# One weight pair in each of eight gate/up blocks: its low part made by an adding DMA or on GpSimd instead of on VectorE

## The chip, the cores and the metric

The kernel is one program on one core of a Trainium2 chip. The metric is the device time of one execution in microseconds (us). A run's time is a little longer than the span of the profiled execution, which goes from the first to the last recorded instruction.

## The reference

A block of a language model, 256 tokens by 2048 features, all in fp32: a feed-forward, a mixer, a second feed-forward, each with a norm ahead of it, a norm behind it and a residual addition.

```python
D_MODEL, SEQ, D_FF = 2048, 256, 5632

def _swiglu(x, w_gate, w_up, w_down):
    return (jax.nn.silu(x @ w_gate) * (x @ w_up)) @ w_down

def reference(x, ...):
    h = x
    f = _swiglu(_rmsnorm(h, ln_ffn1_pre), ffn1_gate, ffn1_up, ffn1_down)
    h = h + 0.5 * _rmsnorm(f, ln_ffn1_post)
    mx = _hybrid_mixer(_rmsnorm(h, ln_mix_pre), ...)   # rwkv7 scan + pooling
    h = h + _rmsnorm(mx, ln_mix_post)
    f = _swiglu(_rmsnorm(h, ln_ffn2_pre), ffn2_gate, ffn2_up, ffn2_down)
    return h + 0.5 * _rmsnorm(f, ln_ffn2_post)
```

The change touches only `x @ w_gate` and `x @ w_up` of the two feed-forwards.

## The kernel before

**Three products for one.** An fp32 product is made of three products of the type float32r. Each operand is split into a high part H (its value rounded to float32r) and a low part L (the value minus H), and `mm3` (L176 to L179) adds H·H, H·L and L·H: the lines L177, L178 and L179 of the profile. L178 is the one that needs the weight's low part.

**A weight's way.** Weights come in pairs: two rows of 128 by 512 columns, 512 KB, one tile of 128x1024. SyncE issues the load (`get_w`, L139), ScalarE casts the high part (`two`, L153), VectorE subtracts to get the low part (L154), and TensorE multiplies. The fp32 tile is one of four buffers (`w32`), the high and the low parts are in rings of five (`wH`, `wL`). Other tiles come from a pool of 33 larger buffers, `unit`.

**Order.** The program works with planned times. `put(t, fn)` appends matmul work that takes t to a list and moves the planned clock `clk`; `at(t, fn)` plans other work for a time; `run` replays both in the order of time. This fixes the order of the instructions on TensorE, ScalarE and VectorE; SyncE and GpSimd issue in the order in which `run` reaches their work. A pair is loaded at `slot(end)`: the planned end of the use that lies five ring entries back, so when its buffers come free. A matmul is planned at `MM` = 0.2265 us.

**A gate/up block.** The 5632 columns are done in 11 blocks of 512. Blocks 0 and 1 multiply plainly. Blocks 2 to 10 (`FAST`) go through `seven`, which saves matmuls by combining gate (called f, first) and up (l, last) weights: two rows of each give a "quad" of seven products in place of eight. A quad needs four loads of 256 KB (L372), three sums on VectorE (L377, L381, L385), casts on ScalarE (L392) and low parts on VectorE (L393). A block is three quads and ten plain pairs, in the order f6, f8, f10, quad, f12, f14, quad, then l6, l8, quad, l10, l12, l14 (the number is the pair's first row). That makes 183 matmuls, 41.5 us. Behind them come the merge (a copy on ScalarE, L416, and additions on VectorE, L419 and L435), the silu on ScalarE (L720) and the product with up on VectorE (L724). The result is turned in blocks of 32 on VectorE (L623), brought to its places by 16 transfers that GpSimd issues in the course of the next block (L635, `x<-T`), and split into high and low (L647, L651). Those transfers are GpSimd's only work in these blocks.

**The pair of the change.** It is l12, the last but one of a block. Its place among the engines' work around it, in order:

- TensorE: quad (second), l6, l8, quad (third), l10, **l12**, l14, next block.
- ScalarE and VectorE: cast and low part of l12 stand some 5 us ahead of its matmuls, behind those of l10.
- SyncE: its load follows the third quad's four loads and that of l10.

Of the kernel before, what the change touches and what calls it, by code (L numbers as in the profile page):

```python
# [11 lines left out]
F32 = mybir.dt.float32  # L12
F32R = mybir.dt.float32r
AF = mybir.ActivationFunctionType
ALU = mybir.AluOpType
# [3 lines left out]
P = 128  # L19
# [18 lines left out]
MM, MC = 0.2265, 0.12  # L38
# [9 lines left out]
        (2, 8, ((2, 4, 6, 8, 10, 12), (0, 2)), TRAIL))  # L48
OUT = ((0, 0, (), 0), (1, 2, ((4,), (0,)), 0), (3, 0, (), TRAIL))
FAST = range(2, 11)  # L50
CARRY = (18, 21)
NG, SPOTS = 3, ((2, 4), (1,))

# [5 lines left out]
class Block:  # L59
# [197 lines left out]
    def sums(s, T, out, when, own=None, nq=2):  # L257
# [62 lines left out]
        for i, fn in enumerate((first, second) + ((parts, lows) if own is not None  # L320
                                                  else (third, fourth))):
            s.at(when + 1.7 * i, fn)

    def seven(s, wf, cf, wl, cl, at, KT, T, sm, n, spots, ev_first, ev_last, trail=0,
              one_end=False, ends=(-0.05, 2.7)):


        nc = s.nc
# [15 lines left out]
        def rows(k, h):  # L344
            xH, xL = at(k)
            return xH[:, h * P:h * P + P], xL[:, h * P:h * P + P]
        ws = {}

        def keep(tiles):
            ws.update((k, (wH, wL)) for k, wH, wL in tiles)  # L350

        def pair(k, w, c0, b):
            s.at(s.slot(s.clk + 12 * MM), lambda: keep(s.load_w(w, k, 2, c0, 512)))

            def do():
                for i in range(2):
                    for h in range(2):
                        mul(f"{b}{h}", rows(k + i, h), ws[k + i])
            s.put(12 * MM, do)
# [265 lines left out]
    def carry_at(s, T1, T, t, x32=None):  # L625
# [34 lines left out]
        for h in range(2):  # L660
            s.at(t + CARRY[h], lambda h=h: high(h))
            s.at(t + CARRY[h] + 2, lambda h=h: low(h))

# [30 lines left out]
    def sumsq(s, src, acc):  # L694
        s.nc.scalar.activation(out=s.rtmp("junk").bitcast(mybir.dt.bfloat16), in_=src, func=AF.Square, accum_out=acc)

    def ffn(s, wg, wu, wd, uT, rs, gpost, resid, emit, reload, xs=None):
        nc = s.nc
        hT, sm = [], []
        at = s.T_at(uT)  # L700
        nb = NKF // 4

        st = {}

        def block(b):
            sig = [None, None]
            T1 = []

            def turned(h, src):
                if not T1:  # L710
                    T1.append(s.unit(p="T1"))
                s.turn(T1[0], h, src)

            def ev_g(h, ps):
                sig[h] = s.tmp("sg")
                nc.scalar.activation(out=sig[h], in_=ps, func=AF.Silu, scale=r[h])

            def ev_f(h, u):
                sig[h] = u
                nc.scalar.activation(out=u, in_=u, func=AF.Silu)  # L720

            def ev_l(o):
                for h in range(2):
                    nc.vector.tensor_tensor(out=o[h], in0=o[h], in1=sig[h], op=ALU.mult)  # L724
                for h in range(2):
                    turned(h, o[h])

            def ev_um(h, ps):
                nc.vector.scalar_tensor_tensor(out=sig[h], in0=ps, scalar=r[h], in1=sig[h],
                                               op0=ALU.mult, op1=ALU.mult)  # L730
                turned(h, sig[h])

            r = rs if b < 2 else [1.0, 1.0]
            if b > 0:
                s.carry_at(*st["T1"], s.clk + 8)
            st["T1"] = (T1, hT)
            if b == 0:
                s.gemm_tok(wg, 0, at, NKD, ev_g, lead=True, xs=xs)
                s.gemm_tok(wu, 0, at, NKD, ev_um, hold=True)
                while s.after:  # L740
                    s.after.pop(0)()
                st["rb"] = s.rtmp("rsb")
                s.spread(rs, st["rb"])
                return
            if b == 1:
                st["nT"], st["su"] = s.normed(uT, st["rb"], s.clk + 4), []
                s.sums(st["nT"], st["su"], s.clk + 16)
                s.sums(st["nT"], st["su"], s.clk + 27, nq=1)
            nT, su = st["nT"], st["su"]
            if b in FAST:  # L750
                s.seven(wg, b * 512, wu, b * 512, s.T_at(nT), NKD, nT, su, NG, SPOTS,
                        ev_f, ev_l, one_end=True)
                return
            x = at if b == 1 else s.T_at(nT)
            s.gemm_at(wg, b * 512, x, NKD, ev_g)
            s.gemm_at(wu, b * 512, x, NKD, ev_um)

        for b in range(nb):
            block(b)
        s.carry_at(*st["T1"], s.clk + 8)  # L760
        s.post(wd, s.T_at(hT), NKF, gpost, 0.5, resid, emit, reload, hT, sm,
               (((3, 2), (24, 2), (40, 2), (76, 2)), {}, DOWN))
# [743 lines left out]
def kernel(tc, x, ln_ffn1_pre, ln_ffn1_post, ffn1_gate, ffn1_up, ffn1_down,  # L1506
                      ln_mix_pre, ln_mix_post, w_in, rwkv_mu, rwkv_w0, rwkv_w2, rwkv_a0,
                      rwkv_a2, rwkv_g2, rwkv_k_k, rwkv_k_a, rwkv_r_k, rwkv_gn_w, rwkv_gn_b,
                      w_proj_a, pool_w, pool_scale, w_proj_b, w_out, ln_ffn2_pre,
                      ln_ffn2_post, ffn2_gate, ffn2_up, ffn2_down, out):  # L1510
    nc = tc.nc
    prm = dict(w_in=w_in[0], mu=rwkv_mu[0], w0=rwkv_w0[0], w2=rwkv_w2[0], a0=rwkv_a0[0],
               a2=rwkv_a2[0], g2=rwkv_g2[0], k_k=rwkv_k_k[0], k_a=rwkv_k_a[0],
               r_k=rwkv_r_k[0].rearrange("h d -> (h d)"), gn_w=rwkv_gn_w[0],
               gn_b=rwkv_gn_b[0], pool_w=pool_w[0], pool_scale=pool_scale[0],
               w_proj_a=w_proj_a[0], w_proj_b=w_proj_b[0], w_out=w_out[0],
               ln_mix_pre=ln_mix_pre[0], ln_ffn2_pre=ln_ffn2_pre[0])
    with ExitStack() as ctx:
        s = Block(tc, ctx)
        xs = [[s.unit(p="x") for _ in range(2)] for _ in range(2)]  # L1520

        def at_tok(u):
            return lambda h, c: u[h][c // 2][:, (c % 2) * 512:(c % 2) * 512 + 512]
        gr = s.rtmp("g1rows")[:16, :P]
        g1 = s.const([P, 16], "g1")
        uT, rs, pre = s.next_pre(lambda: g1)

        def load(h, c):
            if h is None:
                nc.sync.dma_start(out=gr, in_=ln_ffn1_pre[0].rearrange("(k p) -> k p", p=P))  # L1530
                ps = s.psum("pg1")
                nc.tensor.transpose(ps[:, :16], gr, s.ident[:16, :16])
                nc.vector.tensor_copy(g1, ps[:, :16])
                return
            (nc.sync if c else nc.scalar).dma_start(
                out=at_tok(xs)(h, c), in_=x[0, h * P:h * P + P, c * 512:c * 512 + 512])

        def turn(h, c):
            pre(h, c, at_tok(xs)(h, c))
        s.after.append(lambda: s.setup_mixer(prm))  # L1540
        uT2, rs2, pre2 = s.next_pre(lambda: s.col["ln_mix_pre"])
        xr = [[s.unit(p="xr") for _ in range(2)] for _ in range(2)]

        def load_to(dst, src):
            def f():
                for h in range(2):
                    for c in range(2):
                        nc.gpsimd.dma_start(out=dst[h][c],
                                            in_=src(h)[:, c * 1024:c * 1024 + 1024])
            return f  # L1550
        hsp = s.dp.tile([2, 2, P, D], F32, tag="hsp", name="hsp")

        def emit1(h, c, ap, at):
            pre2(h, c, ap, at)
            nc.gpsimd.dma_start(out=hsp[0, h, :, c * 512:c * 512 + 512], in_=ap)
        s.ffn(ffn1_gate[0], ffn1_up[0], ffn1_down[0], uT, rs, ln_ffn1_post[0],
              at_tok(xr), emit1, load_to(xr, lambda h: x[0, h * P:h * P + P]), (load, turn))
        uT3, rs3, pre3 = s.next_pre(lambda: s.col["ln_ffn2_pre"])
        h1 = [[s.unit(p="h1") for _ in range(2)] for _ in range(2)]
        h2 = [[s.unit(p="h2") for _ in range(2)] for _ in range(2)]  # L1560

        def emit2(h, c, ap, at):
            pre3(h, c, ap, at)
            nc.gpsimd.dma_start(out=hsp[1, h, :, c * 512:c * 512 + 512], in_=ap)
        s.mixer(prm, uT2, rs2, at_tok(h1), emit2, ln_mix_post[0],
                load_to(h1, lambda h: hsp[0, h]))

        def emit(h, c, ap, at):
            nc.sync.dma_start(out=out[0, h * P:h * P + P, c * 512:c * 512 + 512], in_=ap)
        s.ffn(ffn2_gate[0], ffn2_up[0], ffn2_down[0], uT3, rs3, ln_ffn2_post[0],  # L1570
              at_tok(h2), emit, load_to(h2, lambda h: hsp[1, h]))
        s.run()


# [30 lines left out]
```

## Time and profile before

| | |
|---|---|
| Runs | 2030.49 and 2030.29 us, median 2030.39 |
| Span of the profiled execution | 2028.3 us; the profiled execution is one of these runs, so 2.0 to 2.2 us lie outside the span |
| TensorE (PE) | busy 2012.7 us, 99% |
| VectorE (DVE) | busy 1746.8 us, 86% |
| ScalarE (ACT) | busy 1159.4 us, 57% |
| GpSimd (POOL) | busy 323.4 us, 16% |
| DMA | 209 GB/s on average |
| Granted TensorE clock | 1.00 in the blocks of the change |
| Blocks 3 to 6 | begin at 140.6, 182.1, 223.5 and 265.0 us (first feed-forward) and at 1456.2, 1497.7, 1539.2 and 1580.6 us (second) |

How to read the rows: "x551 | 660.4, 1211" is 551 instructions, 660.4 us of busy time, 1211 ns for one; behind the second bar stands the idle time of the engine just before them and what ended it. In rows of a timeline the first number is the start in us, the second the duration (of a group, "x2", from its first start to its last end), and the bracket the idle time before and what ended it. Waits are listed as "who waited <- for whom: us in total, times, longest". PE is TensorE's matmul, PEld its weight load, SPq and POOLq are the sequencers that issue DMAs. A matmul is shown with 0.39 us, but one starts every 0.227 us.

### The profile page before, as it was taken

Reading aid. Unit: us, or ns where it says so; the run is one execution under the profiler, and the core shown is the slowest. Engines: PE = TensorE matmul, PEld = TensorE weight load, DVE = VectorE, ACT = ScalarE, POOL = GpSimd, SP = SyncE. Lnnn points to the kernel's source line nnn. Section 1 sums busy time; section 2 is a strip of 40 time slices with the busy share of each in tenths; the row PEclk is TensorE's granted clock in tenths of the full one; section 3 lists DMA queues with packets and bytes.
Section 4 is the critical chain, followed back from the end, with each engine's and each line's share of the span. In section 5 each row is a group of like instructions: output and inputs, shape, how many; then the busy total and the mean of one; then the engine's idle time right before and its main releaser. Section 6 shows DMA issues by size and latency. Waiting matters only on the chain.

```text
span 2028.3 us, 28794 instructions
## 1 busy us (share of the span) xinstructions
PE 2012.7 (99%) x10011; PEld 1664.0 (82%) x10011; DVE 1746.8 (86%) x2304; ACT 1159.4 (57%) x1559; POOL 323.4 (16%) x673
## 2 busy tenths in 40 slices
PE   9999999999999999999999999999999999999997
PEld 7888888888888888888788788888888888888886
DVE  6999999999998867799689577869999999999986
ACT  7555555555555566685576444565555555555553
POOL 0122111221000023413220111001211112110000
PEclk9999999999999999999999999999999999999999
DMA  7667676676667777757556558676676767666674
GB/s 261 192 207 224 218 219 207 209 222 213 197 218 258 224 213 211 203 177 215 148 171 186 160 169 274 206 220 193 202 226 211 227 200 227 217 208 203 213 258 146
DMA packets 226841, 423.55 MB, mean 209 GB/s; under 512 B 24063, under 2 KB 27529, under 8 KB 226697
## 3 DMA queue, kind: packets, MB, share of 16 engines
q1 hardware_dynamic: 204137, 384.70, 61.1%
q0 software_dynamic: 22272, 36.51, 5.5%
q8 instruction: 78, 1.28, 0.3%
q10 hardware_dynamic: 288, 0.52, 0.1%
q14 instruction: 66, 0.54, 0.1%
HBM read 396.69 MB, written 8.39 MB: 200 GB/s over the span
## 4 chain that ended last, share of the span: by engine, by line
PE 97%; issue 1%; DVE 1%; ACT 0%; POOL 0%; DMA 0%; POOLq 0%; DVEq 0%; SPq 0%; ACTq 0%
PE mm L177 27%; PE mm L179 27%; PE mm L178 27%; PE ms L177 4%; PE ms L178 4%; PE ms L179 4%; PE tr L605 1%; PE pA L1326 0%; PE mc L576 0%; PE pU L1422 0%; DMA w<-in_ffn_gate_dram 0%; PE pSa L1434 0%; PE pY L1457 0%; PE pT L1493 0%; PE pM L1392 0%
## 5 line engine op out<-in xcount | busy, mean ns | idle before, releaser
L177 PE MATMUL mm<-wH,xH 128*128 128x512 f32 (+1 forms) x2232 | 870.4, 391 | 0.0
L179 PE MATMUL mm<-wH,xL 128*128 128x512 f32 (+1 forms) x2232 | 866.2, 388 | 0.7 <-DVE xL L613 0.7
L178 PE MATMUL mm<-wL,xH 128*128 128x512 f32 (+1 forms) x2232 | 866.1, 388 | 0.0
L154 DVE TENSOR_TENSOR wL<-w,wH 128x1024 fp32r<-128x1024 f32 (+2 forms) x551 | 660.4, 1211 | 183.3 <-ACT wH L153 175.4
L153 ACT CAST wH<-w 128x1024 fp32r<-128x1024 f32 (+2 forms) x551 | 567.3, 1045 | 351.5 <-PE mm L179 241.9
L179 PEld LDWEIGHTS mm<-wH,xL 128*128 128x128 f32 x2232 | 419.0, 188 | 87.9 <-DVE xL L613 1.5
L177 PEld LDWEIGHTS mm<-wH,xH 128*128 128x128 f32 x2232 | 418.9, 188 | 86.9 <-issue 0.4
L178 PEld LDWEIGHTS mm<-wL,xH 128*128 128x128 f32 x2232 | 419.2, 188 | 83.9 <-DVE wL L154 0.3
L392 ACT CAST wH<-t 128x1024 fp32r<-128x1024 f32 x172 | 181.0, 1054 | 283.8 <-DVE t L385 180.0
L635 POOL DMA_DIRECT2D x<-T x352 | 172.3, 498 | 734.0 <-issue 401.1
L393 DVE TENSOR_TENSOR wL<-t,wH 128x1024 fp32r<-128x1024 f32 x172 | 209.9, 1223 | 11.1 <-ACT wH L392 6.6
L393 DVE TENSOR_TENSOR wL<-w,wH 128x1024 fp32r<-128x1024 f32 (+1 forms) x172 | 163.6, 951 | 1.1 <-ACT wH L392 1.1
L392 ACT CAST wH<-w 128x1024 fp32r<-128x1024 f32 (+1 forms) x172 | 140.4, 832 | 25.6 <-DMA w<-in_ffn_down_dram 13.5
L377 DVE TENSOR_TENSOR t<-w,w 128x1024 f32<-128x1024 f32 x86 | 105.0, 1220 | 2.3 <-DMA w<-in_ffn_down_dram 2.3
L179 PE MATMUL ms<-wH,sL 128*128 128x512 f32 x174 | 67.7, 389 | 0.0
L178 PE MATMUL ms<-wL,sH 128*128 128x512 f32 x174 | 67.7, 389 | 0.0
L177 PE MATMUL ms<-wH,sH 128*128 128x512 f32 x174 | 67.7, 389 | 0.0
L419 DVE TENSOR_TENSOR u<-ms,u 128x512 f32<-128x512 f32 x92 | 61.4, 687 | 1.4
L688 POOL DMA_DIRECT2D R<-R x96 | 47.0, 497 | 84.1 <-issue 72.2
L385 DVE TENSOR_TENSOR t<-w,t 128x512 f32<-128x512 f32 x86 | 59.1, 687 | 0.0
L381 DVE TENSOR_TENSOR t<-w,t 128x512 f32<-128x512 f32 x86 | 59.1, 687 | 0.0
L814 POOL DMA_DIRECT2D gb<-in_ln_ffn_post_dram x4 | 2.2, 557 | 285.0 <-PE mm L179 142.6
(323 smaller groups left out, 1986.1 us busy)
## 6 DMA issues: line engine op xcount, KB each, us to landing
w<-in_w_in_dram SPq DMA_DIRECT2D x128, 512.0 KB
w<-in_ffn_up_dram SPq DMA_DIRECT2D x122, 512.0 KB
w<-in_ffn_gate_dram SPq DMA_DIRECT2D x120, 512.0 KB
w<-in_ffn_down_dram SPq DMA_DIRECT2D x116, 512.0 KB
w<-in_ffn_down_dram SPq DMA_DIRECT2D x120, 256.0 KB
w<-in_ffn_gate_dram SPq DMA_DIRECT2D x112, 256.0 KB
w<-in_ffn_up_dram SPq DMA_DIRECT2D x108, 256.0 KB
w<-in_w_out_dram SPq DMA_DIRECT2D x28, 512.0 KB
```

What stands on the lines that cost most here:

```text
L153: s.nc.scalar.copy(vH, v)
L154: s.nc.vector.tensor_tensor(out=vL, in0=v, in1=vH.bitcast(F32), op=ALU.subtract)
L177: nc.tensor.matmul(ps, aH, bH, start=start, stop=False)
L178: nc.tensor.matmul(ps, aH, bL, start=False, stop=False)
L179: nc.tensor.matmul(ps, aL, bH, start=False, stop=stop)
L377: V.tensor_tensor(out=v["t13"], in0=v["a"], in1=v["b0"].to_broadcast([P, 2, 512]), op=ALU.subtract)
L381: V.tensor_tensor(out=v["t24"][:, 0], in0=v["a"][:, 0], in1=v["t13"][:, 1], op=ALU.add)
L385: V.tensor_tensor(out=v["t24"][:, 1], in0=v["b"][:, 0], in1=v["t24"][:, 0], op=ALU.subtract)
L392: nc.scalar.copy(H, v[n_])
L393: V.tensor_tensor(out=L, in0=v[n_], in1=H.bitcast(F32), op=ALU.subtract)
L419: V.tensor_tensor(out=u[o], in0=bank[b], in1=u[i], op=ALU.add)
L635: nc.gpsimd.dma_start(out=x[0][q * 32:q * 32 + 32, i], in_=src[i * 32:i * 32 + 32, q])
```

## The change

In blocks 3 to 6 (`PROBE`) of both feed-forwards, the pair l12 goes its own way (`low_by`). It is loaded into a buffer of the larger pool 24 us ahead of its planned use; 18 us ahead ScalarE casts the high part into another (dH). The low part goes into a third (dL):

- First feed-forward (`"dma"`): ScalarE writes the negated weight, rounded to float32r, into dL. A DMA issued by GpSimd then adds the fp32 weight to dL.
- Second feed-forward (`"pool"`): GpSimd subtracts dH from the weight.

The pair uses no entry of the rings any more, which moves the later pairs of the ring one slot earlier. The matmuls and their order stay. The new load stands on SyncE behind those of l6 and l8 and ahead of the third quad's; on ScalarE the new work stands behind the second quad's last cast and ahead of the casts of l6 and l8; on GpSimd it stands behind the 16 transfers of the block. Eight subtractions L154 are gone from VectorE.

```diff
+PROBE = range(3, 7)
...
+    def low_by(s, how, w, k, c0, t, keep):
+
+        nc = s.nc
+        x = {}
+
+        def get():
+            x["w"] = s.get_w(w, k, 2, c0, 512, own=True)
+
+        def high():
+            x["H"], x["L"] = s.unit(dt=F32R, p="dH"), s.unit(dt=F32R, p="dL")
+            nc.scalar.copy(x["H"], x["w"])
+            if how == "dma":
+                nc.scalar.activation(out=x["L"], in_=x["w"], func=AF.Copy, scale=-1.0)
+
+        def low():
+            if how == "dma":
+                nc.gpsimd.dma_start(out=x["L"], in_=x["w"], accum_op=ALU.add)
+            else:
+                nc.gpsimd.tensor_tensor(out=x["L"], in0=x["w"], in1=x["H"].bitcast(F32),
+                                        op=ALU.subtract)
+            H, L = [x[n].rearrange("p (k c) -> p k c", k=2) for n in "HL"]
+            keep([(k + i, H[:, i], L[:, i]) for i in range(2)])
+        s.at(t - 24, get)
+        s.at(t - 18, high)
+        s.at(t - 17.9, low)
...
     def seven(s, wf, cf, wl, cl, at, KT, T, sm, n, spots, ev_first, ev_last, trail=0,
-              one_end=False, ends=(-0.05, 2.7)):
+              one_end=False, ends=(-0.05, 2.7), other=None):
...
         def pair(k, w, c0, b):
-            s.at(s.slot(s.clk + 12 * MM), lambda: keep(s.load_w(w, k, 2, c0, 512)))
+            if other and (b, k) == other[1]:
+                s.low_by(other[0], w, k, c0, s.clk, keep)
+            else:
+                s.at(s.slot(s.clk + 12 * MM), lambda: keep(s.load_w(w, k, 2, c0, 512)))
...
                 s.seven(wg, b * 512, wu, b * 512, s.T_at(nT), NKD, nT, su, NG, SPOTS,
-                        ev_f, ev_l, one_end=True)
+                        ev_f, ev_l, one_end=True,
+                        other=(how, ("l", 12)) if b in PROBE else None)
```

The two calls of `ffn` pass `"dma"` and `"pool"`.

More of the change, by code (lines that the diff above doesn't have):

```diff
@@ L695, in sumsq, with ffn @@
         s.nc.scalar.activation(out=s.rtmp("junk").bitcast(mybir.dt.bfloat16), in_=src, func=AF.Square, accum_out=acc)
-    def ffn(s, wg, wu, wd, uT, rs, gpost, resid, emit, reload, xs=None):
+    def ffn(s, wg, wu, wd, uT, rs, gpost, resid, emit, reload, xs=None, how=None):
         nc = s.nc
@@ L1556 @@
         s.ffn(ffn1_gate[0], ffn1_up[0], ffn1_down[0], uT, rs, ln_ffn1_post[0],
-              at_tok(xr), emit1, load_to(xr, lambda h: x[0, h * P:h * P + P]), (load, turn))
+              at_tok(xr), emit1, load_to(xr, lambda h: x[0, h * P:h * P + P]), (load, turn), "dma")
         uT3, rs3, pre3 = s.next_pre(lambda: s.col["ln_ffn2_pre"])
@@ L1570 @@
         s.ffn(ffn2_gate[0], ffn2_up[0], ffn2_down[0], uT3, rs3, ln_ffn2_post[0],
-              at_tok(h2), emit, load_to(h2, lambda h: hsp[1, h]))
+              at_tok(h2), emit, load_to(h2, lambda h: hsp[1, h]), None, "pool")
         s.run()
```

## The prediction

> **What bounds the kernel now.** I read the page's busy shares first, then the chain that ended last, then the waits of TensorE, and then the windows of one changed block of each feed-forward.
>
> ```profile
> span 2028.3 us, 28794 instructions
> PE 2012.7 (99%) x10011; PEld 1664.0 (82%) x10011; DVE 1746.8 (86%) x2304; ACT 1159.4 (57%) x1559; POOL 323.4 (16%) x673
> ...
> PE 97%; issue 1%; DVE 1%; ACT 0%; POOL 0%; DMA 0%; POOLq 0%; DVEq 0%; SPq 0%; ACTq 0%
> ```
> ```profile
> engine line waited for: us in total, times, longest us
> PE warm L484 <- POOL ident masks.py:199: 1.7, 1, 1.7
> PE mm L179 <- DVE xL L613: 0.7, 2, 0.5
> PE pS L1442 <- ACT R L1436: 0.7, 1, 0.7
> PE tr L605 <- DVE fg L846: 0.7, 1, 0.7
> PE tr L605 <- DMA x<-in_x_dram: 0.5, 1, 0.5
> ```
> ```profile
> core 0: us, PE busy (x) PEld busy (x) DVE busy (x) ACT busy (x) POOL busy (x), PEclk, DMA share, GB/s
> 140.60:182.10 41.50, 41.50 (x185) 34.38 (x184) 39.66 (x46) 23.66 (x28) 7.81 (x16) 1.00 0.70 215
> 1456.20:1497.70 41.50, 41.50 (x185) 34.38 (x184) 39.63 (x46) 23.62 (x28) 7.82 (x16) 1.00 0.70 215
> ```
>
> TensorE (PE) is the bound, at the full granted clock (1.00). It is busy for 2012.7 of 2028.3 us and carries 97% of the chain. All its waits together are 4.3 us, and none of the five lines is in a gate/up block. The two windows are block 3 of the first and of the second feed-forward: 41.5 us long, PE busy for 41.5. VectorE (DVE) is close behind with 39.7, ScalarE (ACT) has 23.7, GpSimd (POOL) 7.8. So DVE has 1.8 us to spare in a block, PE nothing, and making DVE's work smaller can't shorten a block in which PE never waits. What the change can do is make PE wait.
>
> **What it removes.** Each changed block loses one low-part subtraction on DVE:
>
> ```profile
> L154 DVE TENSOR_TENSOR wL<-w,wH 128x1024 fp32r<-128x1024 f32 (+2 forms) x551 | 660.4, 1211 | 183.3 <-ACT wH L153 175.4
> L153 ACT CAST wH<-w 128x1024 fp32r<-128x1024 f32 (+2 forms) x551 | 567.3, 1045 | 351.5 <-PE mm L179 241.9
> ```
>
> That is 8 x 1.21 = 9.7 us of DVE work. PE waits for none of it in these blocks, so it is worth 0 us; if DVE and not PE set a block's length, it would be worth up to 9.7. PE's instructions and their order are unchanged. The pair also leaves the weight rings, so the pairs after it are loaded one slot earlier: 0 us, for the same reason.
>
> **What it moves.** The cast to the high part is not new, but it stands much earlier on ACT, about 16 us ahead of its use instead of about 5. Built, its place is right behind the second up-quad's last cast (L392) and ahead of the casts (L153) of gate pairs l6 and l8 (these come next; the changed pair is l12). Its load moves too: it stands on SP behind the loads of l6 and l8 and ahead of the next quad's four. In the first feed-forward ACT gets a second operation there, the negated copy. So the question is whether l6 still comes in time. The rows of the first feed-forward, block 3, from the timelines of SP, ACT, DVE and PE:
>
> ```profile
> start us, us, engine line op out<-in xcount [idle before <-releaser]
> 152.28 1.51 SPq L139 DMA_DIRECT2D w<-in_ffn_up_dram  x2
> 157.58 1.05 ACT L392 CAST wH<-t 128x1024 fp32r<-128x1024 f32 x1 [1.89 <-DVE t L385]
> 158.96 1.05 ACT L153 CAST wH<-w 128x1024 fp32r<-128x1024 f32 x1 [0.33 <-PE mm L179]
> 160.04 2.59 DVE L154 TENSOR_TENSOR wL<-w,wH 128x1024 fp32r<-128x1024 f32 x2 [0.16 <-ACT wH L153]
> 163.70 0.39 PE L178 MATMUL mm<-wL,xH 128*128 128x512 f32 x1
> 176.62 0.39 PE L178 MATMUL mm<-wL,xH 128*128 128x512 f32 x1
> ```
> ```profile
> 153.00:157.50 4.50, 4.50 (x21) 3.72 (x21) 4.50 (x7) 1.66 (x2) 2.87 (x6) 1.00 0.95 284
> 157.50:159.00 1.50, 1.50 (x9) 1.23 (x8) 1.44 (x2) 1.09 (x2) 0.00 (x0) 1.00 0.98 299
> ```
>
> The two loads issued from 152.28 on are 1,024 KB. From 153.0 to 157.5 the DMA engines move 284 GB/s x 4.5 us = 1.28 MB, 0.2 of it the 32 KB transfers on POOL's queue, so l6 and l8 have landed at about 157.4 (estimate; the rows have the columns of the windows above). The new 512 KB behind them take 0.52 MB / 299 GB/s = 1.75 us: landed at 159.1. The high cast then runs at 159.1 to 160.1 (ACT is free from 158.6), the negated copy to 161.1, and l6's cast goes at 161.1 instead of 158.96: 2.1 us late. Its low part was ready at 160.04 + 1.22 = 161.26 for a matmul at 163.70, 2.4 us ahead; 0.3 us are left, of which the weight load into the array (about 0.2) takes most. Stall about 0, and 0 to 0.6 per block if the landing is half a microsecond later. What follows on DVE goes 1.2 to 1.6 us later; the next low parts stand further ahead of PE, and DVE has one subtraction less soon after. First feed-forward: 0 taken, range 0 to 2.4 for four blocks.
>
> **The adding DMA.** POOL issues it when the negated copy is there, at 161.1; PE needs it at 176.62, so it has 15.3 us. Behind it on POOL stand the next block's transfers, over 20 us later. No adding DMA is in the trace. The nearest are POOL's 512 KB transfers and its small ones:
>
> ```profile
> x<-T POOLq DMA_DIRECT2D x352, 32.0 KB, 3.5
> h<-hsp POOLq DMA_DIRECT2D x8, 512.0 KB, 6.5
> gb<-in_ln_mix_post_dram POOLq DMA_DIRECT2D x2, 512.0 KB, 8.6
> ```
>
> Lower end: a plain transfer, 6.5 us, hidden. Upper end: sixteen 32 KB pieces one after another, 16 x 3.5 = 56 us. I take twice the plain one, as it has to read its destination too: 13 us, to 17.2 by the slower row, a stall of 0 to 1.9 us a block. It is nearest in size to the 512 KB rows, so 0 is taken.
>
> **The GpSimd subtraction.** Second feed-forward, block 3:
>
> ```profile
> 1472.98 2.51 DVE L393 TENSOR_TENSOR wL<-t,wH 128x1024 fp32r<-128x1024 f32 x2
> 1475.66 2.59 DVE L154 TENSOR_TENSOR wL<-w,wH 128x1024 fp32r<-128x1024 f32 x2 [0.16 <-ACT wH L153]
> 1474.57 1.05 ACT L153 CAST wH<-w 128x1024 fp32r<-128x1024 f32 x1 [0.34 <-PE mm L179]
> 1479.31 0.39 PE L178 MATMUL mm<-wL,xH 128*128 128x512 f32 x1
> ```
> ```profile
> 1469.00:1473.00 4.00, 4.00 (x20) 3.30 (x19) 4.00 (x6) 1.67 (x2) 2.47 (x6) 1.00 0.96 302
> 1473.00:1474.50 1.50, 1.50 (x8) 1.27 (x7) 1.44 (x3) 1.05 (x1) 0.00 (x0) 1.00 0.96 311
> ```
>
> By the same walk l6 and l8 have landed at about 1473.0 and the new 512 KB at 1473.0 + 1.7 = 1474.7; the high cast ends at 1475.7, l6's cast at 1476.7, 1.1 us later than before. POOL's subtraction starts at about 1475.8, in the moment in which DVE waits for l6's cast. That matters because the two engines exclude each other:
>
> ```profile
> 975.27 1.22 POOL L1426 COPY R<-R 64x256 f32<-64x256 f32 x1 [5.68 <-PE pX L1402]
> 976.56 0.40 POOL L1427 COPY R<-R 64x256 f32<-64x256 f32 x1
> 975.01 1.23 DVE L154 TENSOR_TENSOR wL<-w,wH 128x1024 fp32r<-128x1024 f32 x1 [1.78 <-ACT wH L153]
> 985.15 0.40 POOL L1426 COPY R<-R 64x256 f32<-64x256 f32 x1 [8.20 <-PE pS L1442]
> 985.19 0.64 DVE L951 TENSOR_TENSOR zv<-zv,zb 128x256 f32<-128x256 f32 x1
> L951 DVE TENSOR_TENSOR zv<-zv,zb x8: 384/425/641, 846.9 to 985.2; 128x256 f32<-128x256 f32 x8
> ```
>
> A copy of 0.40 us on POOL took 1.22 when L154 had begun just ahead of it, and the DVE addition of L951 took 0.64 instead of 0.43 (its median) when POOL's copy had begun just ahead. Whoever comes second waits for the end of the first.
>
> The Trainium skill, "SBUF — State Buffer", "Who interferes with whom", says the same, for DVE instructions with two SBUF inputs against GpSimd's reads; that speaks against this part of the change, and these rows agree (1.22 against 0.40).
>
> The size: no 128x1024 subtraction is on POOL. The copy of 256 elements at 0.40 us gives 4 x 0.40 = 1.6 us for 1024, one input (lower end, 1.2 with a share that doesn't grow); the double for two inputs is 3.2. The trace has POOL tensor operations of another kind, a power:
>
> ```profile
> 1037.22 2.90 POOL L1248 TENSOR_TENSOR n<-n,mhalf 128x16 f32<-128x16 f32 x1 [19.10 <-DVE n L1246]
> ```
>
> At 0.18 us an element it would be 185 us for 1024; that is the far upper end, and as a subtraction is nearer to a copy than to a power I don't use it. I take the middle of 1.6 and 3.2: 2.4 us, so POOL holds DVE from 1475.8 to 1478.2, l6's low part is ready at 1478.2 + 1.22 = 1479.4, and PE's weight load wants it at 1479.1. Stall 0.3 us; with 1.6 none, with 3.2 it is 1.1, and with 4.5 (a copy's rate doubled once more, less a fixed part) 2.4. All four blocks have the same order: 4 x 0.3 = 1.2 us.
>
> The Trainium skill, "GPSIMD Engine Reference", section 3.1, has 4.5 us for an fp32 addition of 2048 elements, which gives an estimate of 2.25 for 1024, and would make the sum 0.6 instead of 1.2; no run here shows it yet.
>
> **Sum.** Span 2028.3; the run's time was 2030.5 or 2030.3 (median 2030.39), so 2.1 us lie outside the span. Removed 0, moved 0, adding DMA 0, POOL against DVE +1.2: 2029.5 in the span, 2031.6 us.
>
> **Rivals.**
> 1. Nothing at all is seen: all the added work lies in covers. For it: POOL is 81% idle in these blocks, and l6 has 2.4 us of lead. Against: ACT's and POOL's chain, as walked, uses that lead up. 2030.4 us.
> 2. The subtraction on POOL takes 3.2 to 4.5 us. Then 1.1 to 2.4 us a block: 2035 to 2040. For: two inputs double the copy's price. Against: nothing but the copies' rate.
> 3. ACT is held in order by the new load. DMA engines run at 0.95 to 0.98 there, and the load stands ahead of four quad loads. If it lands 1 us later than I have it, l6 is late by 0.7 in the first feed-forward and 1.3 in the second: 8 us, 2038. Against: the rates above are those of just these stretches.
> 4. The other side, slower: the adding DMA moves in small pieces. It decides from 15.3 us of landing on; 25.4 us make 4 x 10.1 = 40.6 us, 2%. At the 32 KB rate (56 us) it is 4 x 40.7 = 163: 2193 us; at half of that, 28 us, 2081. For: no adding DMA is in the trace. Against: 512 KB rows of the same queue land in 6.5 to 8.6.
> 5. Faster: the relief of DVE shortens the blocks. At most 9.7 us (2020.7), and only if PE waited for DVE there, which no row shows.
>
> **How the numbers follow.** Forecast (2031 to 2033) 0.44; nothing seen 0.2; 2 and 3 together 0.2; the DMA between 17 and 25 us (2037 to 2071) 0.08; beyond 25 us 0.06; faster 0.02, within 2% as well. Two per cent, 40.6 us, is about what a measurement of this kernel tells from no change. So: faster by over 2% 0.01, within 0.93, slower 0.06. The range goes from 2029.6 (0.8 below before, for small gains) to 2040.0, the end of rival 2; beyond it lie about 15 in 100.
>
> **What would show it.** Right: PE busy for the whole of the 41.5 us windows in the first feed-forward; in the second, waits of PE for DVE's l6 low part (L154) of some 0.3 us, one a block; DVE's busy time in these windows down by 1.2 but up by waits beside POOL; POOL's subtraction at 2 to 3 us. Wrong: PE's L178 waits for a DMA, which is rival 4; PE waits in the first feed-forward for L154, rival 3; a time under 2029.6, which would mean that PE had been held by something that I haven't seen.

## The result, and the profile after

The changed kernel takes 2051.43 us (median of 2049.53 and 2053.32) against 2030.39 before: ratio 1.0103, interval 1.0074 to 1.0133. It is 21 us slower, outside the range of the prediction (2029.6 to 2040.0), though within 2%. The profiled execution is the one of 2049.53 us.

The page after, busy shares and chain:

```profile
span 2047.8 us, 28810 instructions
PE 2019.4 (99%) x10011; PEld 1664.0 (81%) x10011; DVE 1741.7 (85%) x2296; ACT 1161.5 (57%) x1563; POOL 337.8 (16%) x681
...
PE 81%; DVE 8%; issue 4%; DMA 3%; ACT 2%; POOL 0%; DVEq 0%; ACTq 0%; POOLq 0%; SPq 0%
```

VectorE's busy time is 5.1 us lower (1741.7 against 1746.8; that is less than the 9.7 removed, at least in part because time in which GpSimd holds it counts as busy), and 8% of the chain now runs through it, where it was 1%. (The new file's lines stand 1 to 31 further down: L154 is now L155, L153 is L154, L392 is L422, L419 is L449, L1302 is L1333.) The waits of TensorE after (us in total, times, longest), in three stretches: the first feed-forward from block 3 on, the mixer, and blocks 3 to 6 of the second feed-forward with the start of the next:

```profile
PE mm L178 <- DVE u L449: 2.0, 5, 0.6
PE mm L179 <- DVE wL L155: 1.6, 3, 0.8
PE mm L178 <- ACT wH L154: 0.5, 1, 0.5
...
PE pA L1357 <- DVE R L1333: 1.3, 2, 1.1
PE pB L1376 <- DVE R L1368: 1.1, 2, 0.8
...
PE mm L178 <- ACT sgb L994: 0.6, 1, 0.6
...
PE mm L179 <- DVE wL L155: 3.4, 3, 1.9
PE mm L178 <- DVE u L449: 1.6, 3, 0.9
```

There are three kinds of new waits: for a weight's parts (L155, L154), for the merge additions (L449), and in the mixer (L1333, L1368, L994), which nobody edited. To size them I matched the matmuls of the two traces one by one (10011 in both, in the same order) and read off how much later each one starts. 3.5 us come at l6 in the first feed-forward and 3.0 at block starts there; 3.7 in the mixer; in the second feed-forward 4.2 at l6, 2.4 at block starts, and 1.7 in a slow stretch behind the longest wait, where seven matmuls started 427 ns apart instead of 227 and a few at its edges were slower too. Together with 0.3 us at the program's start that is 18.8 of the 19.5 us between the spans.

**How l6 came late.** Timelines after, first feed-forward, block 3 (SP, ACT, DVE, PE):

```profile
152.60 2.06 SPq L140 DMA_DIRECT2D w<-in_ffn_up_dram  x3
157.89 1.05 ACT L422 CAST wH<-t 128x1024 fp32r<-128x1024 f32 x1 [1.89 <-DVE t L415]
160.58 1.05 ACT L335 CAST dH<-w 128x1024 fp32r<-128x1024 f32 x1 [1.64 <-DMA w<-in_ffn_up_dram]
161.54 1.05 ACT L337 ACTIVATE dL<-w 128x1024 fp32r<-128x1024 f32 x1
162.50 1.98 ACT L154 CAST wH<-w 128x1024 fp32r<-128x1024 f32 x2
163.56 2.36 DVE L155 TENSOR_TENSOR wL<-w,wH 128x1024 fp32r<-128x1024 f32 x2 [3.36 <-ACT wH L154]
164.85 0.50 PE L179 MATMUL mm<-wL,xH 128*128 128x512 f32 x1 [0.69 <-DVE wL L155]
```

The chain is the one that the prediction walked, but the changed pair's load landed at 160.6 and not at 159.1 (0.3 of these 1.5 us are the later start of the program). ScalarE, free since 158.9, waited 1.64 us for it, and the cast of l6 stood behind. Over blocks 3 to 6 this wait adds up:

```profile
ACT dH L335 <- DMA w<-in_ffn_up_dram: 7.2, 4, 2.9
```

What SyncE's queue (q1) moved from 152.6 to 160.5 us, in packets, MB and share of the DMA engines:

```profile
q1 hardware_dynamic: 983, 1.89, 74.4%
```

The loads of l6, l8 and the changed pair are 1.57 MB together, and the trace has no packet of an older load in this queue between 152.6 and 153.5. So 0.3 MB of the quad loads issued behind them had been moved before the changed pair's load was complete.

**How the block start came late.** At the end of block 3, DVE before, then ACT, DVE and PE after:

```profile
176.35 1.23 DVE L154 TENSOR_TENSOR wL<-w,wH 128x1024 fp32r<-128x1024 f32 x1 [0.54 <-ACT wH L153]
177.49 2.73 DVE L419 TENSOR_TENSOR u<-ms,u 128x512 f32<-128x512 f32 x4
180.15 1.28 DVE L419 TENSOR_TENSOR u<-mm,u 128x512 f32<-128x512 f32 x2
181.34 1.21 DVE L154 TENSOR_TENSOR wL<-w,wH 128x1024 fp32r<-128x1024 f32 x1
...
177.91 1.05 ACT L154 CAST wH<-w 128x1024 fp32r<-128x1024 f32 x1 [1.91 <-PE mm L180]
179.00 1.23 DVE L155 TENSOR_TENSOR wL<-w,wH 128x1024 fp32r<-128x1024 f32 x1 [0.76 <-ACT wH L154]
180.14 2.73 DVE L449 TENSOR_TENSOR u<-ms,u 128x512 f32<-128x512 f32 x4
182.79 1.28 DVE L449 TENSOR_TENSOR u<-mm,u 128x512 f32<-128x512 f32 x2
183.62 0.47 PE L178 MATMUL mm<-wH,xH 128*128 128x512 f32 x1 [0.35 <-DVE u L449]
```

Before, the low part of the next block's f10 was made behind the merge (181.34). After, with a ring entry free, it stands ahead of it (179.00), some 10 us before TensorE needs it. The merge additions begin 2.65 us later, 1.4 of them against TensorE, which is 1.25 us late itself by then. One of the last two (`u<-mm`), which frees the accumulator that the next block begins with, now ends after TensorE wants it.

### The profile page after: what moved, and what is told of

The parts are those of the page before. It is cut to its first block, busy times and chain, and to the rows that moved or that the text cites. A ratio compares the mean times of both kernels' runs of the same rounds, so it can differ in the third digit from the quotient of the medians.

```text
span 2047.8 us, 28810 instructions
## 1 busy us (share of the span) xinstructions
PE 2019.4 (99%) x10011; PEld 1664.0 (81%) x10011; DVE 1741.7 (85%) x2296; ACT 1161.5 (57%) x1563; POOL 337.8 (16%) x681
## 4 chain that ended last, share of the span: by engine, by line
PE 81%; DVE 8%; issue 4%; DMA 3%; ACT 2%; POOL 0%; DVEq 0%; ACTq 0%; POOLq 0%; SPq 0%
PE mm L178 23%; PE mm L180 23%; PE mm L179 23%; PE ms L179 3%; PE ms L180 3%; PE ms L178 3%; DVE wL L155 2%; DMA w<-in_ffn_gate_dram 2%; DVE u L449 1%; DMA w<-in_ffn_up_dram 1%; ACT wH L154 1%; DVE t L407 1%; DVE wL L423 1%; ACT wH L422 1%; PE tr L635 1%
## 5 line engine op out<-in xcount | busy, mean ns | idle before, releaser
L178 PE MATMUL mm<-wH,xH 128*128 128x512 f32 x2200 | 859.4, 391 | 4.8 <-DVE u L449 3.7
L179 PE MATMUL mm<-wL,xH 128*128 128x512 f32 x2200 | 855.3, 389 | 5.0 <-DVE wL L155 5.0
L180 PE MATMUL mm<-wH,xL 128*128 128x512 f32 x2200 | 854.6, 388 | 0.7 <-DVE xL L643 0.7
L155 DVE TENSOR_TENSOR wL<-w,wH 128x1024 fp32r<-128x1024 f32 (+1 forms) x543 | 655.2, 1220 | 205.7 <-ACT wH L154 199.6
L154 ACT CAST wH<-w 128x1024 fp32r<-128x1024 f32 (+1 forms) x543 | 557.9, 1044 | 342.5 <-PE mm L180 245.1
L178 PEld LDWEIGHTS mm<-wH,xH 128*128 128x128 f32 x2200 | 413.4, 188 | 94.4 <-issue 6.8
L179 PEld LDWEIGHTS mm<-wL,xH 128*128 128x128 f32 x2200 | 413.5, 188 | 90.6 <-DVE wL L155 8.3
L180 PEld LDWEIGHTS mm<-wH,xL 128*128 128x128 f32 x2200 | 413.4, 188 | 86.2 <-DVE xL L643 1.5
L422 ACT CAST wH<-t 128x1024 fp32r<-128x1024 f32 x172 | 181.1, 1054 | 291.9 <-DVE t L415 172.0
L423 DVE TENSOR_TENSOR wL<-w,wH 128x1024 fp32r<-128x1024 f32 (+1 forms) x172 | 163.1, 948 | 1.1 <-ACT wH L422 1.1
L422 ACT CAST wH<-w 128x1024 fp32r<-128x1024 f32 (+1 forms) x172 | 140.6, 832 | 30.5 <-DMA w<-in_ffn_down_dram 15.3
L449 DVE TENSOR_TENSOR u<-ms,u 128x512 f32<-128x512 f32 x92 | 61.4, 686 | 1.4
```

What stands on the lines that cost most here:

```text
L154: s.nc.scalar.copy(vH, v)
L155: s.nc.vector.tensor_tensor(out=vL, in0=v, in1=vH.bitcast(F32), op=ALU.subtract)
L178: nc.tensor.matmul(ps, aH, bH, start=start, stop=False)
L179: nc.tensor.matmul(ps, aH, bL, start=False, stop=False)
L180: nc.tensor.matmul(ps, aL, bH, start=False, stop=stop)
L422: nc.scalar.copy(H, v[n_])
```

## The experiments

One table for all: time and ratio against before, and how much later than before TensorE's matmuls run at the end of each stretch than at its beginning (us, from the matched matmuls of the profiled execution; the 0 to 3 us of the program's start and up to 0.4 between 306 and 640 us are left out).

| kernel | us | ratio (interval) | blocks 3-6, first | mixer | second |
|---|---|---|---|---|---|
| changed | 2051.43 | 1.0103 (1.0074 to 1.0133) | 6.1 | 3.65 | 8.4 |
| e1 adding DMA alone | 2042.08 | 1.0053 (1.0038 to 1.0068) | 7.3 | 3.80 | 0.0 |
| e2 GpSimd alone | 2041.15 | 1.0048 (1.0033 to 1.0063) | 0.0 | 0.03 | 8.9 |
| e3 cast later | 2039.17 | 1.0041 (1.0027 to 1.0055) | 0.2 | 3.67 | 4.1 |
| e4 ring entry counted | 2044.80 | 1.0066 (1.0051 to 1.0081) | 4.9 | 3.69 | 5.1 |
| e5 both of these | 2034.96 | 1.0020 (1.0010 to 1.0029) | 0.0 | 4.16 | 0.0 |
| e6 mixer's order kept | 2049.25 | 1.0086 (1.0069 to 1.0103) | 6.7 | 0.01 | 12.1 |
| e7 load earlier | 2035.77 | 1.0026 (1.0016 to 1.0036) | 0.0 | 3.69 | 1.1 |
| e8 low part on VectorE | 2043.46 | 1.0061 (1.0046 to 1.0076) | 7.1 | 0.03 | 5.4 |
| e9 e7 + ring + mixer | 2030.95 | 1.0002 (0.9993 to 1.0011) | 0.0 | 0.02 | 0.0 |
| e10 e7 + mixer | 2032.58 | 1.0010 (1.0002 to 1.0019) | 0.0 | 0.01 | 1.4 |
| e11 adding DMA in both | 2051.10 | 1.0098 (1.0083 to 1.0113) | 7.9 | 3.64 | 9.5 |
| e12 GpSimd in both | 2054.08 | 1.0110 (1.0093 to 1.0127) | 10.6 | 3.91 | 9.3 |

**e1 and e2: each half alone.** The other feed-forward gets `how = None`, and its pair goes the old way.

```diff
-        other=(how, ("l", 12)) if b in PROBE else None)
+        other=(how, ("l", 12)) if how and b in PROBE else None)
```

> The change in the first feed-forward alone (adding DMA); the second feed-forward is as before. Theory: of the 19 us that TensorE is later at the end of the changed kernel, 6.5 us come in the first feed-forward (the changed pair's load lands late and holds ScalarE's casts of l6; f10's cast and subtraction stand ahead of the block's merge) and 3.7 us in the mixer, where VectorE's and ScalarE's instructions are in another order, though nothing was edited there. So 2030.4 + 10.2 = about 2040.5, with the mixer 3.7 us late as in the changed kernel. Rival (the mixer's loss has to do with the second feed-forward or is chance): about 2037, mixer at its time of before.

> The change in the second feed-forward alone (GpSimd's subtraction). Theory: the 8.3 us of the second feed-forward stay and nothing else: about 2038.7; first feed-forward and mixer at their times of before. Rival (the second feed-forward suffers only because it starts in another state, after a delayed first part): close to 2031.

Measured 2042.1 and 2041.2, some 2 us above both expectations, but stretch by stretch as the theory had it: each half pays in its own feed-forward, and the mixer's loss comes with the first half, to the size.

**e3: the cast later.**

```diff
-        s.at(t - 18, high)
-        s.at(t - 17.9, low)
+        s.at(t - 14, high)
+        s.at(t - 13.9, low)
```

> The changed kernel with the high cast (and the negated copy) planned 14 us ahead of use instead of 18, and the adding DMA or GpSimd's subtraction with it. On ScalarE they then stand behind the casts of l6 and l8, so the changed pair's load, however late, holds nothing that TensorE needs at once. Theory (late landing holds ScalarE in order): the waits of TensorE for l6's low part and the slower clock behind the longest of them go, 3.5 us in the first and 5.9 us in the second feed-forward; the block-start waits (5.4 us) and the mixer (3.7) stay: 2049.5 - 9.4 = about 2040. Rival (the traffic of the adding DMA, and GpSimd excluding VectorE, make the waits): these stay in size and only move: 2048 to 2051.

2039.2, near the 2040 of the theory, though not all of its parts came out. Behind the casts of l6 and l8 the late load holds nothing: TensorE waits for no low part in either feed-forward. The block-start waits, which I expected to stay, went in the first feed-forward and grew in the second:

```profile
PE mm L178 <- DVE u L449: 0.2, 1, 0.2
...
PE mm L178 <- DVE u L449: 2.9, 4, 1.1
```

**e4: the ring entry counted in the plan.**

```diff
-                s.low_by(other[0], w, k, c0, s.clk, keep)
+                s.slot(s.clk + 12 * MM), s.low_by(other[0], w, k, c0, s.clk, keep)
```

> The changed kernel, with the ring entry that the changed pair no longer uses still counted in the plan, so that all pairs behind it are loaded at the planned times of before. Theory (f10's early cast and subtraction stand ahead of the merge and so delay the additions that free TensorE's accumulators): the waits of TensorE for a merge addition at the block starts go, 3.0 + 2.4 = 5.4 us; the l6 waits and the mixer stay: 2049.5 - 5.4 = about 2044. Rival (the block-start waits are a later echo of the l6 wait, VectorE being behind since then): they stay, 2048 to 2051.

2044.8, as expected. First and second feed-forward in this kernel:

```profile
PE mm L179 <- DVE wL L155: 2.5, 4, 0.8
PE mm L178 <- ACT wH L154: 0.6, 1, 0.6
PE mm L178 <- DVE u L449: 0.2, 1, 0.2
...
PE mm L179 <- DVE wL L155: 4.2, 3, 1.6
```

The waits for the merge are gone, those for l6 are there. With e3 this says that the block-start wait needs two things: f10's low part ahead of the merge, and VectorE late, by l6 or (as e3's second feed-forward suggests) by GpSimd's subtraction. The traces of the first feed-forward show it for block 3: the first `u<-mm` addition ends, against the time at which TensorE wants it, 1.6 us ahead where only l6 is late (e4), 0.3 ahead where only f10 stands early (e7), and 0.4 behind with both (the changed kernel).

**e5: e3 and e4 together.**

> Both cures at once: high cast at 14 us ahead of use, and the ring entry counted. Theory: both kinds of waits in the two feed-forwards go and only the mixer's 3.7 us are left: 2030.4 + 3.7 = about 2034. Rival (the waits have a common cause that neither removes): over 2038.

2035.0. Nothing is left in either feed-forward, though adding DMAs, GpSimd subtractions and the added casts are all there; only the mixer's part remains.

**e6: the mixer's order.** In the mixer the source fixes by hand the order of TensorE alone; that of VectorE and ScalarE is worked out when the program is built. In the traces their order there differs from that of before in every kernel that has taken one subtraction a block from VectorE in the first feed-forward and put nothing in its place; why it then comes out otherwise is not shown. A small copy per block (0.42 us, where 0.7 was expected) tips it back:

```diff
-        s.at(t - 17.9, low)
+        s.at(t - 17.9, low); s.at(t - 5, lambda: nc.vector.tensor_copy(s.tmp("dz"), x["w"][:, :512]))
```

> The changed kernel with one small copy on VectorE (128x512, its result is not used) added 5 us ahead of the changed pair's use in each changed block. VectorE has lost a 1.2 us subtraction in the same block, so 0.7 us more has room. With it, the mixer's instructions stand in the order of before. Theory (the mixer's loss is its order): 2049.5 - 3.7 = about 2046, and the mixer at its length of before. Rival (the mixer is later because of what reaches it from the first feed-forward): no gain in the mixer.

The mixer's loss is gone (0.01 us), as the theory said; over all kernels, the five whose traces have VectorE's and ScalarE's order of before in the mixer (e2, e6, e8, e9, e10) lose 0.01 to 0.03 us there, the eight others, which have the order of the changed kernel, 3.6 to 4.2. The whole fell to 2049.25 only, not to 2046, as the second feed-forward lost 12.1 us in this execution instead of 8.4: its waits vary with the landing of the loads (in block 6 the high cast began 2.4 us later than the prediction walked, in the changed kernel 0.2 earlier). What the other order did in the mixer, DVE and PE, before and then after:

```profile
894.85 0.68 DVE L1302 TENSOR_TENSOR R<-R,R 64x512 f32<-64x512 f32 x1
895.46 0.47 DVE L1156 SCALAR_TENSOR_TENSOR yb<-mc,cols,yb 128x256 fp32r<-128x256 f32 x1
895.85 1.21 DVE L154 TENSOR_TENSOR wL<-w,wH 128x1024 fp32r<-128x1024 f32 x1
897.09 0.69 DVE L1302 TENSOR_TENSOR R<-R,R 64x512 f32<-64x512 f32 x1
897.50 0.37 PE L1326 MATMUL pA<-R,R 64*128 64x128 f32 x1
...
904.16 1.23 DVE L155 TENSOR_TENSOR wL<-w,wH 128x1024 fp32r<-128x1024 f32 x1
905.30 0.48 DVE L1187 SCALAR_TENSOR_TENSOR yb<-mc,cols,yb 128x256 fp32r<-128x256 f32 x1
905.70 1.39 DVE L1333 TENSOR_TENSOR R<-R,R 64x512 f32<-64x512 f32 x2
906.52 0.34 PE L1357 MATMUL pA<-R,R 64*128 64x128 f32 x1 [1.09 <-DVE R L1333]
```

Before, one of these products of `R` (L1302) ran ahead of the weight's low part and one behind it; after, both stand behind it, and TensorE's matmul waits 1.09 us for the first.

**e7: the load earlier.**

```diff
-        s.at(t - 24, get)
+        s.at(t - 30, get)
```

> The changed kernel with the changed pair's load planned 30 us ahead of use instead of 24: on SyncE it stands ahead of the loads of l6 and l8 and away from the quad's. The work on ScalarE stays where it is. Theory (it is the landing, not the 1 or 2 us of added ScalarE work, that makes l6 late): the high cast starts about 2 us earlier, TensorE's waits for l6 in the first feed-forward go (3.5 us), and those of the second shrink to what GpSimd's 2.4 us leave (up to 1 us a block): 2049.5 - 3.5 - 3 = about 2043. Rival (ScalarE's added work alone uses the lead up): 2048 to 2051.

2035.8, far below the 2043 expected. ACT and DVE of the first feed-forward, block 3, then ACT, POOL and DVE of the second:

```profile
158.60 1.05 ACT L335 CAST dH<-w 128x1024 fp32r<-128x1024 f32 x1
160.51 1.98 ACT L154 CAST wH<-w 128x1024 fp32r<-128x1024 f32 x2
161.57 2.36 DVE L155 TENSOR_TENSOR wL<-w,wH 128x1024 fp32r<-128x1024 f32 x2 [1.62 <-ACT wH L154]
...
1477.71 1.05 ACT L335 CAST dH<-w 128x1024 fp32r<-128x1024 f32 x1
1478.84 2.49 POOL L343 TENSOR_TENSOR dL<-w,dH 128x1024 fp32r<-128x1024 f32 x1 [3.76 <-ACT dH L335]
1479.74 3.81 DVE L155 TENSOR_TENSOR wL<-w,wH 128x1024 fp32r<-128x1024 f32 x2 [0.68 <-ACT wH L154]
```

The high cast now follows the quad's cast without a wait, and the same added work on ScalarE costs nothing in the first feed-forward. It is the landing that made l6 late. With l6 in time the block-start waits are gone too, but for 0.3 us in the second feed-forward, which is where I had expected too much; that fits what e3 and e4 say together.

**e8: the low part on VectorE.**

```diff
-                nc.gpsimd.tensor_tensor(out=x["L"], in0=x["w"], in1=x["H"].bitcast(F32),
+                nc.vector.tensor_tensor(out=x["L"], in0=x["w"], in1=x["H"].bitcast(F32),
```

(and `"pool"` passed in both feed-forwards)

> The changed kernel with the low part made on VectorE in both feed-forwards, at the place in the plan where GpSimd or the adding DMA would make it: neither a GpSimd subtraction nor an adding DMA nor a negated copy, but the same early load, high cast and ring. The mixer is in the order of before. Theory (the place, not the engine, costs): TensorE waits for l6 in both feed-forwards; with the low part of the changed pair ahead of l6's on VectorE, 0.5 to 1.5 us a block, and at the block starts as in the changed kernel: 2036 to 2044. Rival (the adding DMA and GpSimd are the cause): within 1 us of 2030.4.

2043.5: the same waits without a GpSimd subtraction, an adding DMA or a negated copy. So neither of the two new ways is needed for the loss; the place in the plan is enough. (Here VectorE's own 1.2 us for the changed pair stand ahead of l6's low part.)

**e9 and e10: all causes away, and all but the ring.** e9 is e7 with the edits of e4 and e6, e10 is e7 with that of e6.

> All three causes taken away, with the adding DMA, GpSimd's subtraction and ScalarE's added work kept at their places: the load 30 us ahead, the ring entry counted, and the small copy on VectorE that keeps the mixer's order. Theory: nothing is left, 2030.7 (the time of before in these comparisons), within 0.5 us; it can't be faster, as TensorE has no wait to give back. Rival (the added operations have a price of their own): 2 us or more above before.

> As the run before it, but with the ring entry not counted, as in the changed kernel. Theory (f10's earlier place costs only where VectorE is late, which in the second feed-forward it still is by GpSimd's 2.4 us): the first feed-forward and the mixer as before, 1 us in the second: about 2031.7. Rival (the earlier place costs by itself at each block's start): 5 us more, 2036.

Both as expected. e9 can't be told from before (1.0002, 0.9993 to 1.0011), with every operation of the change still in it. (Its profiled execution lost 3.2 us at the program's start, where TensorE waited 1.4 us for the first input and then had a granted clock of 0.50 from 8.45 to 15.2 us.) So the added operations have no price of their own that this measurement can tell (the interval's upper end is 2.2 us), and the relief of VectorE has no worth: e9 leaves it 0.8 us a block, e5, without the copies, the whole 1.2, and neither gains in the feed-forwards.

**e11 and e12: one way in both.**

> The changed kernel with the adding DMA in both feed-forwards. Theory (the late load is common to both ways, and GpSimd's subtraction adds to it by holding VectorE for some 1.4 us): the second feed-forward loses about what the first does, 6 to 7 us instead of 8 to 12: about 2030.4 + 6.5 + 3.7 + 6.5 = 2047. Rival (the second feed-forward loses more for another reason than GpSimd): 2049 to 2053 as the changed kernel.

> The changed kernel with GpSimd's subtraction in both feed-forwards. Same theory: the first feed-forward then loses what the second does, 8 to 12 us instead of 6 to 7: 2051 to 2057. Rival: the first stays at 6 to 7, 2050.

e11 went to the rival: with the adding DMA the second feed-forward loses 9.5 us, no less than with GpSimd's subtraction (8.4 to 12.1). e12's first feed-forward loses 10.6; 1.7 of it is slowed matmuls behind one long wait, and the other 8.9 compare with 6.1 to 7.9 in the four kernels with the adding DMA at this place (changed, e1, e6, e11). So GpSimd's hold on VectorE is there (3.73 us for two subtractions that take 2.36 in the same place without it). But what it costs against the adding DMA, with its second ScalarE operation ahead of l6, stays open: in the second feed-forward no difference is shown, and the one in the first rests on a single execution, in which the load of the first changed block landed 2.9 us later than walked (1.2 to 2.0 in the four others).

## Why the prediction was wrong

- **What bounds the kernel** held: TensorE has nothing to give back. e9, with 8 subtractions fewer on VectorE (and 8 shorter copies more), is no faster, and e5, without the copies, gains nothing in the feed-forwards.
- **The adding DMA** held. I took 13 us to landing, an estimate with no adding DMA in the trace. It took 5.0, well within its 15 us, so the stall of 0 was right though the size was not:

```profile
L343 POOL TENSOR_TENSOR dL<-w,dH x4: 2392/2408/2412, 1487.4 to 1617.6; 128x1024 fp32r<-128x1024 f32 x4
...
DMA to landing us min/median/max: 5.0/5.0/5.5
```

- **GpSimd's subtraction** held in size, 2.41 us against 2.4. That it came so near is partly luck, as 2.4 was the middle between 1.6 and 3.2. Its exclusion of VectorE held too: 1.4 us in the row 1488.30 below. The Trainium skill, "SBUF — State Buffer", "Who interferes with whom", has a VectorE instruction with two SBUF inputs contend with a GpSimd instruction that reads SBUF, and calls the shared ports an exclusive lock. Here that agrees: GpSimd's subtraction runs from 1487.40 to 1489.81, and DVE's first subtraction, begun at 1488.30, ends at 1490.89, 2.6 us instead of 1.2.

```profile
1486.27 1.05 ACT L335 CAST dH<-w 128x1024 fp32r<-128x1024 f32 x1 [1.49 <-DMA w<-in_ffn_up_dram]
1487.40 2.41 POOL L343 TENSOR_TENSOR dL<-w,dH 128x1024 fp32r<-128x1024 f32 x1 [5.36 <-ACT dH L335]
1488.30 3.73 DVE L155 TENSOR_TENSOR wL<-w,wH 128x1024 fp32r<-128x1024 f32 x2 [2.27 <-ACT wH L154]
1490.95 0.50 PE L179 MATMUL mm<-wL,xH 128*128 128x512 f32 x1 [1.02 <-DVE wL L155]
```

- **The landing of the moved load is the first step that failed.** I let it land in turn at the rate of the windows, 159.1; the high cast began at 160.58, and in the eight blocks 0.2 us earlier to 2.2 later than walked, about 1 later on average (each set against its block's own delay). Put 160.58 into the same walk and l6's low part is ready at 164.8, for a matmul that was due at 164.0: a stall of 0.8, against 0.85 by which it moved. The walk was right but for this term. The rate was right and the turn was wrong: by the trace's packets SyncE's queue had moved the 1.57 MB of the three loads at 159.5, 18.6 us behind the block's beginning for 18.5 walked. But the four quad loads, issued from 156.7 on, shared the engines with them. In all eight blocks the queue had moved 1.8 to 2.3 MB when the high cast began, 0.8 to 2.1 us behind the 1.57 MB. The Trainium skill, "DMA: Bandwidth & Descriptors", "Queues, rings and completion order", says that completion is not in order of issue for one issuing engine; this load, which took 6 us from its issue, fits that. No run here takes the quad loads away; e7, which takes the load away from them, has it land in time. Rival 3 had this mechanism, a late load that holds ScalarE in order, and gave it 8 us for 1 us of lateness; measured are 7.7, and 1.7 more for the slowed matmuls. The sign that the prediction gave for it, waits in the first feed-forward for the low part, is there. Rivals 2 and 3 together had a chance of 0.2.
- **"One slot earlier: 0 us" is the second.** I looked at whether TensorE waits for those pairs, and not at what is queued behind them: the merge, whose first `u<-mm` addition ended at about 180.8 before, for a matmul at 181.84. That 1.0 us was the cover, and it was too small for f10's 1.2 us ahead of the merge on a VectorE that a late l6 had kept back. Measured 5.4 us, though not by the earlier slot alone: with l6 in time (e10) the first feed-forward loses nothing and the second 1.4.
- **The third was left out altogether.** The mixer's instructions on VectorE and ScalarE came out in another order, visible in the built program, and the prediction, which follows the change through its own blocks only, has no term for it: 3.7 us, a fifth of the whole.
- The chances: the largest, 0.44, was on a stall of 0.3 us a block in the second feed-forward alone. Each of the three terms was counted at 0 or as a tail, and they add up, which the range did not allow for.

## What to carry to other kernels

Where one engine is busy to the last and the others are fed in a fixed order, look at what an early operation stands ahead of, not only at whether it is itself in time: a cast that waits for a late load holds everything behind it in order. Freeing an engine or a buffer moves later work forward, and what it overtakes can be the work that was due first. Compare the instruction order of the whole program, also far from the edit, and give each difference a term.

## What the runs showed of the hardware

After a longer wait TensorE ran at half the granted clock for a while. PE and windows of the changed kernel, second feed-forward, block 5:

```profile
1578.16 0.50 PE L179 MATMUL mm<-wL,xH 128*128 128x512 f32 x1 [1.94 <-DVE wL L155]
...
1578.15:1579.00 0.85, 0.84 (x4) 0.69 (x5) 0.85 (x1) 0.00 (x0) 0.00 (x0) 1.00 0.00 0
1579.00:1582.30 3.30, 3.30 (x9) 2.55 (x8) 3.30 (x5) 1.05 (x1) 0.00 (x0) 0.51 0.90 259
```

The wait of 1.94 us is 2.33 from start to start; 0.9 us later the clock is 0.51 for some 3.3 us, and seven matmuls start 427 ns apart instead of 227: 1.4 us more, 1.7 with those at the edges of the stretch. In the runs above three waits inside the feed-forwards, of 2.33, 2.51 (e6) and 2.59 us (e12) from start to start, were followed by this; those of 2.15 us and less were not. No wait between 2.15 and 2.33 us was seen. I had expected no cost beyond the wait. The Trainium skill, "TensorE: Matmul & The Clock Gate", "Part 1: The HAM clock gate", has the clock halved after an idle window of about 3.4 us; here shorter waits were enough.
